# All tiles of a depthwise convolution as TensorE products, in a four-layer decoder trunk

## The chip, the cores and the metric

The kernel runs on one core of a Trainium2 chip. The metric is the device time of one launch in microseconds. A core has TensorE (PE, matrix products into PSUM), VectorE (DVE), ScalarE (ACT), GpSimd (POOL) and the sync engine (SP), which issues transfers. Each engine takes its instructions in order and waits on semaphores that others raise.

## The reference

Four pre-norm residual layers over 512 tokens of 1024 channels, in float32. Each is a token mixer followed by a squared-ReLU MLP of 4096 hidden channels; a last RMSNorm ends it. Layer 0 and 3 mix by sliding-window attention, layer 2 by a gated linear recurrence, layer 1 by the convolution module that the change touches:

```python
u = h @ w_pw1 + b_pw1                       # 1024 -> 2048
a, gate = jnp.split(u, 2, axis=-1)
u = a * jax.nn.sigmoid(gate)
c = causal_depthwise_conv(u, w_dw) + b_dw   # 31 taps, each channel by itself
c = jax.nn.silu(layer_norm(c, ln_g, ln_b))  # over the 1024 channels
return c @ w_pw2 + b_pw2
```

## The kernel before

Activations are kept transposed, channels on partitions: eight tiles of 128 channels by 512 tokens. Every large product is made of three matmuls on high and low parts of its operands; one such triple is a step (`step`, L271, matmuls at L277 to L279). After each step `pump` (L130) gives one turn to every live task, a Python generator whose `yield n` skips n turns. So tasks spread the work of other engines, and small TensorE products, among the steps; when the steps are over, `finish` (L140) gives turns until no task is left. This fixes the order in which instructions are written; a scheduler then orders each engine's list by that order and by when operands are expected to be ready. Weights are fetched ahead by the steps (`prefetch`, L256), rounded on ScalarE (wh) and subtracted on VectorE (wl), both at L254.

The convolution layer is `conformer` (L817). `linear` (L286) makes 16 output tiles of 8 steps, in pairs: for channel tile j first the gate, then the value. `glu` (L906) takes each from PSUM on VectorE (L909), applies the sigmoid on ScalarE (L912) and multiplies (L918). Then the tile goes one of two ways.

- Tiles 0 to 2 are convolved on VectorE by the task `on_dve` (L863): one ScalarE instruction for the last tap and 30 multiply-adds of the shifted tile (L872) each, written at a pace of one in 2.4 steps while steps last.
- Tiles 3 to 7 go to TensorE by a task `on_pe` (L887) each. Sixteen ScalarE copies (L891) bring the tile into a layout in which 32 channels by 4 neighbouring tokens lie on the partitions; after LAG (16) turns four groups follow, one per 32 channels. A group (`Convolution.group`, L807) is nine matmuls (L812) against a weight of 34 tap positions by 32 channels, three matmuls a turn; four ScalarE copies (L898) bring each group's result back.

The weights of a group are built on VectorE from a table of taps (`build`, L796, instruction at L802); the table is filled by `prepare` (L782, copies at L790), which starts after 16 turns and builds AHEAD (10) of them.

A shift per token, the mean of tile 0's channels (L856), is subtracted from all tiles (L860, L883, L901). `sums` (L832) adds each finished tile and its square to accumulators on GpSimd (L847, L848); the last but one to finish is added on VectorE, and its end starts `most`, which takes the means of the accumulators on TensorE (L393). The last one's means follow after `finish`. From them come mean and inverse deviation per token (L933 to L939), the normalised tiles (L954 to L958), and the projection `project` (L318), whose first step waits for the first of these.

Of the kernel before, what the change touches and what calls it, by code (L numbers as in the profile page):

```python
# [8 lines left out]
F32 = mybir.dt.float32  # L9
F32R = mybir.dt.float32r  # L10
I32 = mybir.dt.int32
AF = mybir.ActivationFunctionType
ALU = mybir.AluOpType
AX = mybir.AxisListType

P = 128
D = 1024
T = 512
KC = D // P
# [5 lines left out]
CW = 31  # L25
FF = 4 * D
EPS = 1e-6
SLAB = 256
CONV_ON_PE = 5
PACE = 2.4  # L30
LAG = 16
FAR = 1.0e34
W_BUFS = 5
U_BUFS = 3
# [18 lines left out]
def trunk_kernel(  # L53
# [7 lines left out]
    sc, ve, gp, pe = nc.scalar, nc.vector, nc.gpsimd, nc.tensor  # L61
# [12 lines left out]
    def ps_aux():  # L74
        return psa.tile([P, T], F32, tag="aux", name="aux")

    def scratch(name, shape=(P, T), dt=F32):
        return tmp.tile(list(shape), dt, tag="t", name=name)
# [18 lines left out]
    vrows = {}  # L97
# [18 lines left out]
    vecT = const.tile([P, KC, n_rows], F32, name="vecT")  # L116

    def vec(key, j, i=0):
        r = vrows[key] + i
        return vecT[:, j, r : r + 1]  # L120
# [3 lines left out]
    clock = [0]  # L124

    def spawn(gen):

        tasks.append([0, gen])
# [277 lines left out]
    class Norm:  # L406


        def __init__(self, key, i):
            self.key, self.i = key, i  # L410
            self.xs, self.r, self.r2 = [], None, None
            self.ms = tmp.tile([P, 2, NB], F32, tag="ms", name="ms", bufs=2)
            self.n = [0, 0]
# [350 lines left out]
    class Convolution:  # L764

        AHEAD = 10
        TAPS = CW + 3
        DIST = -(-TAPS // 4)  # L770

        def __init__(self):
            cp = self.pool = tc.tile_pool(name="cv", bufs=1)
            self.cp = cp.__enter__()
            self.built = []
            self.taps = self.cp.tile([P, CONV_ON_PE, 4, self.TAPS], F32, name="taps")
            self.i4 = self.cp.tile([P, 32], F32, name="i4")

        def close(self):
            self.pool.__exit__(None, None, None)  # L780

        def prepare(self):  # L782
            yield 16
            j0, r0 = KC - CONV_ON_PE, vrows["w_dw"]
            ve.tensor_reduce(self.i4, ident.rearrange("p (r c) -> p c r", r=4), AX.X, ALU.add)
            ve.memset(self.taps, 0.0)
            yield 2
            for g in range(4):
                for r in range(4):
                    ve.tensor_copy(self.taps[32 * r : 32 * r + 32, :, g, r : r + CW], vecT[32 * g : 32 * g + 32, j0:, r0 + CW - 1 : r0 - 1 : -1])  # L790
                yield 2
            for _ in range(self.AHEAD):
                self.build()
                yield 3

        def build(self):  # L796
            n = len(self.built)
            if n == 4 * CONV_ON_PE:
                return
            nx = self.TAPS  # L800
            w = self.cp.tile([P, nx, 32], F32, tag="w", name="w", bufs=self.AHEAD)
            ve.tensor_tensor(  # L802
                w, self.i4.unsqueeze(1).broadcast_to([P, nx, 32]), self.taps[:, n // 4, n % 4, :].unsqueeze(2).broadcast_to([P, nx, 32]), ALU.mult
            )
            self.built.append(w.rearrange("p x c -> p (x c)"))
# [9 lines left out]
                    yield 1  # L815

    def conformer(i, norm, nxt, conv):  # L817
        ON_DVE = KC - CONV_ON_PE
        cp = conv.cp
        cs, us = {}, {}  # L820
        done, parts, means, shared = [], [], {}, {}
        spawn(norm.inverse_root())

        def most():
            yield 6
            means["ps"] = ps_aux()
            token_means(means["ps"][:, :NB], shared["acc1"])
            token_means(means["ps"][:, NB : 2 * NB], shared["acc2"])
            means["most"] = tiny("most", 2 * NB)
            ve.tensor_copy(means["most"], means["ps"][:, : 2 * NB])  # L830

        def sums(j):  # L832

            done.append(j)
            if len(done) == 1:
                for k in ("acc1", "acc2"):
                    shared[k] = tmp.tile([P, T], F32, tag="acc", name=k, bufs=2)
                gp.tensor_copy(shared["acc1"], cs[j])
                sc.activation(shared["acc2"], cs[j], AF.Square)
                return  # L840
            sq = scratch("csq")
            sc.activation(sq, cs[j], AF.Square)
            if len(done) == KC:
                parts.extend((cs[j], sq))
                return
            e = ve if len(done) == KC - 1 else gp
            e.tensor_tensor(shared["acc1"], shared["acc1"], cs[j], ALU.add)  # L847
            e.tensor_tensor(shared["acc2"], shared["acc2"], sq, ALU.add)  # L848
            if len(done) == KC - 1:
                spawn(most())  # L850

        def first_shift():

            yield 4
            ps = ps_aux()
            pe.matmul(ps, ones, cs[0], start=True, stop=True)  # L856
            shift = shared["shift"] = tmp.tile([P, T], F32, tag="r", name="shift", bufs=2)
            sc.mul(shift, ps, 1.0 / P)
            yield 2
            ve.tensor_tensor(cs[0], cs[0], shift, ALU.subtract)  # L860
            sums(0)

        def on_dve():  # L863
            due = 0
            for j in range(ON_DVE):
                while j not in us:
                    yield 1
                c, u, b = cs[j], us[j], vec("b_dw", j)
                sc.activation(c, u, AF.Identity, scale=vec("w_dw", j, CW - 1), bias=b)
                for k in range(CW - 1):  # L870
                    late = CW - 1 - k
                    ve.scalar_tensor_tensor(c[:, late:], u[:, : T - late], vec("w_dw", j, k), c[:, late:], ALU.mult, ALU.add)  # L872
                    due = max(due + PACE, clock[0])
                    while clock[0] < due and len(us) < KC:
                        yield 1
                    if len(us) == KC:
                        yield 1
                if j == 0:
                    spawn(first_shift())
                    continue  # L880
                while "shift" not in shared:
                    yield 1
                ve.tensor_tensor(c, c, shared["shift"], ALU.subtract)  # L883
                sums(j)
                yield 1

        def on_pe(j, t):  # L887
            u = us[j].rearrange("p (g m) -> p g m", g=4)
            for g in range(4):
                for r in range(4):  # L890
                    sc.copy(u[32 * r : 32 * r + 32, g, :], t[32 * g : 32 * g + 32, r::4])  # L891
            yield LAG
            for g in range(4):
                ps = ps_aux()[:, :P]
                yield from conv.group(ps, 4 * (j - ON_DVE) + g, u[:, g, :])
                conv.build()
                for r in range(4):
                    sc.copy(cs[j][32 * g : 32 * g + 32, r::4], ps[32 * r : 32 * r + 32, :])  # L898
            while "shift" not in shared:
                yield 1  # L900
            ve.scalar_tensor_tensor(cs[j], cs[j], vec("b_dw", j), shared["shift"], ALU.add, ALU.subtract)  # L901
            sums(j)

        gates = {}

        def glu(n, ps):  # L906
            j, jj = n // 2, n % 2
            t = scratch("a")
            ve.tensor_tensor(t, ps, norm.factor(), ALU.mult)  # L909
            if jj == 0:  # L910
                gate = cp.tile([P, T], F32, name="gate", bufs=2)
                sc.activation(gate, t, AF.Sigmoid, bias=vec("b_pw1", j, 1))  # L912
                gates[j] = gate
                return
            uc = xcp.tile([P, 2, T], F32, tag="xc", name="uc")
            us[j], cs[j] = uc[:, 0, :], uc[:, 1, :]
            u = us[j] if j < ON_DVE else t
            ve.scalar_tensor_tensor(u, t, vec("b_pw1", j, 0), gates[j], ALU.add, ALU.mult)  # L918
            if j >= ON_DVE:
                spawn(on_pe(j, t))  # L920

        spawn(on_dve())
        linear(norm.xs, KC, glu, lead=KC - 1)
        for b in range(NB):
            gp.dma_start(out=rows[:, b, :], in_=conv_b_pw2[i].partition_broadcast(P), accum_op=ALU.add)
# [3 lines left out]
        ps = means["ps"]  # L929
# [237 lines left out]
    for c in range(XQ):  # L1167
        cs = slice(c * D // XQ, (c + 1) * D // XQ)
# [34 lines left out]
    for i in range(DEPTH):  # L1203
        mid = Norm("norm_mlp", i)
        if i % 3 == 0:
            attention(i // 3, norm, mid)
        elif i % 3 == 1:
            conv = Convolution()
            spawn(conv.prepare())
            conformer(i // 3, norm, mid, conv)  # L1210
            conv.close()
        else:
            hgrn(i // 3, i, norm, mid)
        norm = Norm("norm_mixer", i + 1) if i + 1 < DEPTH else None
        mlp(i, mid, norm)
# [31 lines left out]
```

## Time and profile before

| | us |
|---|---|
| median of three runs (2179.83 to 2183.03) | 2181.76 |
| the profiled execution | 2179.59 |
| its span, first to last instruction | 2177.8 |
| TensorE busy | 2122.2 |
| VectorE busy | 1418.3 |
| ScalarE busy | 1156.9 |
| GpSimd busy | 200.5 |

The profile is of one execution. Times of instructions are microseconds from the start of the span. TensorE's matmuls are pipelined: the durations of neighbours overlap, so the distance of their starts is what one costs. A float32 matmul appears as two records. PEld is the load of the stationary operand, which overlaps matmuls. PEclk is the clock that was granted to TensorE, as a share of the full 2.4 GHz, averaged over the stretch.

### The profile page before, as it was taken

How to read it: one execution, taken by the hardware profiler on the slowest of the kernel's cores; microseconds unless marked ns; L12 is line 12 of the kernel's file. 1: busy time of each engine (PE TensorE's matmuls, PEld its weight loads, DVE VectorE, ACT ScalarE, POOL GpSimd, SP SyncE). 2: the span in 40 equal slices, each digit the busy share in tenths (PEclk: the TensorE clock that was granted, in tenths of full speed). 3: DMA queues.
4: the chain of work that ended last, by engine and by line, in shares of the span. 5: the costliest groups of instructions: out<-in, count | busy, mean ns of one | idle time of the engine just before them, and what ended most of it. 6: DMA issues, size and time to landing. Idle time of an engine off the chain costs nothing.

```text
span 2177.8 us, 27270 instructions
## 1 busy us (share of the span) xinstructions
PE 2122.2 (97%) x10226; PEld 1742.0 (80%) x10226; DVE 1418.3 (65%) x2250; ACT 1156.9 (53%) x2015; POOL 200.5 (9%) x193
## 2 busy tenths in 40 slices
PE   7999999999988999999999999999999999999997
PEld 6778888888877888888788888888888878788886
DVE  5863754759986375574888874547558784547547
ACT  6755453455685445445555554544546684534545
POOL 0000110110020011011300000101100000101100
PEclk9999999999999999999999999999999999999999
DMA  4144756745214375674322226567564216567553
GB/s 149 49 146 111 187 117 157 177 84 126 78 40 135 97 174 110 170 172 94 87 66 78 77 70 174 111 169 173 109 170 88 61 48 195 114 158 177 120 129 77
DMA packets 211063, 262.56 MB, mean 121 GB/s; under 512 B 9027, under 2 KB 136003, under 8 KB 210932
## 3 DMA queue, kind: packets, MB, share of 16 engines
q1 hardware_dynamic: 175540, 191.61, 27.9%
q0 software_dynamic: 35392, 69.21, 20.1%
q8 instruction: 81, 1.33, 0.2%
q14 instruction: 50, 0.41, 0.1%
HBM read 258.69 MB, written 2.10 MB: 120 GB/s over the span
## 4 chain that ended last, share of the span: by engine, by line
PE 63%; DVE 18%; issue 8%; DMA 6%; ACT 5%; SPq 0%; POOL 0%; DVEq 0%; ACTq 0%; POOLq 0%
PE mm L279 18%; PE mm L278 18%; PE mm L277 18%; DVE wl L254 7%; DMA raw<-in_mlp_w_dram 5%; DVE rows L583 3%; DVE ul L544 2%; ACT wh L254 2%; PE aux L733 2%; PE aux L683 1%; PE aux L1047 1%; ACT uc L891 1%; DVE uc L872 1%; PE aux L428 1%; DVE us L538 1%
## 5 line engine op out<-in xcount | busy, mean ns | idle before, releaser
L254 DVE TENSOR_TENSOR wl<-raw,wh 128x1024 fp32r<-128x1024 f32 x452 | 552.7, 1223 | 532.5 <-ACT wh L254 530.1
L254 ACT CAST wh<-raw 128x1024 fp32r<-128x1024 f32 x452 | 468.7, 1048 | 497.3 <-DMA raw<-in_mlp_w_dram 198.3
L277 PE MATMUL mm<-x,wh 128*128 128x512 f32 x1568 | 630.6, 402 | 9.2 <-ACT wh L254 9.2
L279 PE MATMUL mm<-x,wl 128*128 128x512 f32 x1568 | 615.0, 392 | 7.6 <-DVE wl L254 7.6
L278 PE MATMUL mm<-x,wh 128*128 128x512 f32 x1568 | 613.4, 391 | 0.0
L279 PEld LDWEIGHTS mm<-x,wl 128*128 128x128 f32 x1568 | 294.7, 188 | 74.3 <-DVE wl L254 12.1
L277 PEld LDWEIGHTS mm<-x,wh 128*128 128x128 f32 x1568 | 295.4, 188 | 68.2 <-ACT wh L254 9.5
L278 PEld LDWEIGHTS mm<-x,wh 128*128 128x128 f32 x1568 | 295.6, 188 | 56.4 <-issue 1.4
L217 POOL DMA_DIRECT2D raw<-in_mlp_w_dram x128 | 153.5, 1206 | 1781.3 <-DVE wl L254 891.4
L277 PE MATMUL mm<-wh,uh 128*128 128x512 f32 x768 | 302.5, 394 | 7.1 <-DVE rows L583 4.7
L278 PE MATMUL mm<-wl,uh 128*128 128x512 f32 x768 | 299.2, 390 | 0.0
L279 PE MATMUL mm<-wh,ul 128*128 128x512 f32 x768 | 297.4, 390 | 0.3 <-DVE ul L544 0.3
L277 PEld LDWEIGHTS mm<-wh,uh 128*128 128x128 f32 x768 | 144.1, 188 | 45.8 <-DVE rows L583 7.5
L279 PEld LDWEIGHTS mm<-wh,ul 128*128 128x128 f32 x768 | 144.1, 188 | 31.2 <-DVE ul L544 0.8
L278 PEld LDWEIGHTS mm<-wl,uh 128*128 128x128 f32 x768 | 144.3, 188 | 28.0
L549 ACT ACTIVATE relu<-mm 128x512 f32<-128x512 f32 x128 | 75.9, 593 | 160.2 <-PE mm L279 160.2
L544 DVE TENSOR_TENSOR ul<-us,uh 128x1024 fp32r<-128x1024 f32 x64 | 78.2, 1222 | 32.5 <-ACT uh L543 32.5
L583 DVE SCALAR_TENSOR_TENSOR rows<-mm,nr,rows 128x512 f32<-128x512 f32 x128 | 95.8, 749 | 0.0
L550 ACT ACTIVATE us<-relu 128x512 f32<-128x512 f32 x128 | 81.0, 633 | 4.0
L277 PE MATMUL mm<-wh,y 128*128 128x512 f32 x192 | 77.6, 404 | 0.7 <-ACT y L358 0.7
L416 ACT ACTIVATE sq<-rows 128x512 f32<-128x512 f32 x64 | 40.2, 629 | 69.7 <-DVE rows L330 55.2
L279 PE MATMUL mm<-wh,y 128*128 128x512 f32 x192 | 76.2, 398 | 0.0
(232 smaller groups left out, 2559.5 us busy)
## 6 DMA issues: line engine op xcount, KB each, us to landing
raw<-in_mlp_w_dram SPq DMA_DIRECT2D x256, 512.0 KB
raw<-in_mlp_w_dram POOLq DMA_DIRECT2D x128, 512.0 KB, 6.1
raw<-in_hgrn_w_qfig_dram SPq DMA_DIRECT2D x64, 256.0 KB
raw<-in_attn_w_qkv_dram SPq DMA_DIRECT2D x20, 512.0 KB
raw<-in_attn_w_o_dram SPq DMA_DIRECT2D x16, 512.0 KB
raw<-in_conv_w_pw_dram SPq DMA_DIRECT2D x32, 256.0 KB
raw<-in_conv_w_pw_dram SPq DMA_DIRECT2D x8, 512.0 KB
raw<-in_hgrn_w_o_dram SPq DMA_DIRECT2D x8, 512.0 KB
```

The source lines that it names most:

```text
L217: gp.dma_start(out=wide(to), in_=block(w, r, c, h), accum_op=ALU.add)
L254: return sc.copy(wh, raw), ve.tensor_tensor(wl, raw, wh.bitcast(F32), ALU.subtract)
L277: pe.matmul(ps, sh, mh, start=start, stop=False, skip_group_check=again)
L278: pe.matmul(ps, sh, ml, start=False, stop=False, skip_group_check=again)
L279: pe.matmul(ps, sl, mh, start=False, stop=stop, skip_group_check=again)
L416: sc.activation(scratch("sq"), rows[:, b, f * T : (f + 1) * T], AF.Square, accum_out=self.ms[:, f, b : b + 1])
L428: pe.transpose(ps[:, b * P : (b + 1) * P], rows[:, b, j * P : (j + 1) * P], ident)
L544: ve.tensor_tensor(flat[1], src, flat[0].bitcast(F32), ALU.subtract)
L549: sc.activation(s, ps, AF.Relu)
L550: sc.activation(us[j // KH][:, :, j % KH, :], s.rearrange("p (h t) -> p h t", h=2), AF.Square)
L583: ve.scalar_tensor_tensor(o, banks[bank][p], norm.r2[sign][:, b : b + 1], o, ALU.mult, ALU.add)
L733: pe.matmul(po[h * HD : (h + 1) * HD, n * P : (n + 1) * P], vtok[:, n - 1 + b, kv * HD : (kv + 1) * HD], pT[:, b, n - n0, h, :], start=b = ...
```

## The change

All eight tiles go through `on_pe`; `on_dve`, the constant CONV_ON_PE and its pace are removed. The tap table and the weights cover eight tiles (32 builds instead of 20); 8 instead of 10 are built ahead, and the preparation starts after 4 turns instead of 16. LAG is 10 instead of 16. Of the sixteen layout copies of a tile those for the second and fourth 32 channels go to GpSimd; for the last tile half of the copies, into the layout and back, go to VectorE and half to ScalarE. Tile 0 gets its bias by a VectorE instruction of its own and starts the shift.

```diff
-CONV_ON_PE = 5
-PACE = 2.4
-LAG = 16
+LAG = 10
...
-        AHEAD = 10
+        AHEAD = 8
...
-            self.taps = self.cp.tile([P, CONV_ON_PE, 4, self.TAPS], F32, name="taps")
+            self.taps = self.cp.tile([P, KC, 4, self.TAPS], F32, name="taps")
...
-            yield 16
-            j0, r0 = KC - CONV_ON_PE, vrows["w_dw"]
+            yield 4
+            r0 = vrows["w_dw"]
...
-        def on_dve():
...
         def on_pe(j, t):
             u = us[j].rearrange("p (g m) -> p g m", g=4)
+            ends = j == KC - 1
             for g in range(4):
                 for r in range(4):
-                    sc.copy(u[32 * r : 32 * r + 32, g, :], t[32 * g : 32 * g + 32, r::4])
+                    o, src = u[32 * r : 32 * r + 32, g, :], t[32 * g : 32 * g + 32, r::4]
+                    if ends and r % 2:
+                        ve.tensor_copy(o, src)
+                    elif ends or g % 2 == 0:
+                        sc.copy(o, src)
+                    else:
+                        gp.tensor_copy(o, src)
             yield LAG
             for g in range(4):
                 ps = ps_aux()[:, :P]
-                yield from conv.group(ps, 4 * (j - ON_DVE) + g, u[:, g, :])
+                yield from conv.group(ps, 4 * j + g, u[:, g, :])
                 conv.build()
                 for r in range(4):
-                    sc.copy(cs[j][32 * g : 32 * g + 32, r::4], ps[32 * r : 32 * r + 32, :])
+                    o, src = cs[j][32 * g : 32 * g + 32, r::4], ps[32 * r : 32 * r + 32, :]
+                    if ends and r % 2:
+                        ve.tensor_copy(o, src)
+                    else:
+                        sc.copy(o, src)
+            if j == 0:
+                ve.tensor_scalar(cs[0], cs[0], vec("b_dw", 0), None, ALU.add)
+                spawn(first_shift())
+                return
...
-            u = us[j] if j < ON_DVE else t
-            ve.scalar_tensor_tensor(u, t, vec("b_pw1", j, 0), gates[j], ALU.add, ALU.mult)
-            if j >= ON_DVE:
-                spawn(on_pe(j, t))
-
-        spawn(on_dve())
+            ve.scalar_tensor_tensor(t, t, vec("b_pw1", j, 0), gates[j], ALU.add, ALU.mult)
+            spawn(on_pe(j, t))
+
         linear(norm.xs, KC, glu, lead=KC - 1)
```

## Rows read from the trace of the kernel before

**Rows 1.** The page, first part: busy time, share of the span, instructions.
```profile
PE 2122.2 (97%) x10226; PEld 1742.0 (80%) x10226; DVE 1418.3 (65%) x2250; ACT 1156.9 (53%) x2015; POOL 200.5 (9%) x193
```

**Rows 2.** Stretches: length, PE, PEld, DVE, ACT, POOL busy (x), clock, DMA.
```profile
506.40:626.70 120.30, 119.53 (x628) 99.58 (x627) 115.98 (x161) 74.29 (x146) 12.14 (x9) 1.00 0.34 88
626.70:636.10 9.40, 9.37 (x73) 8.07 (x71) 6.05 (x8) 7.44 (x14) 4.91 (x3) 1.00 0.13 34
636.10:645.00 8.90, 0.00 (x0) 0.00 (x0) 8.68 (x10) 7.81 (x20) 1.94 (x2) 0.79 0.24 82
645.00:657.50 12.50, 12.49 (x72) 10.69 (x72) 7.59 (x8) 9.78 (x25) 3.31 (x2) 0.74 0.01 1
657.50:673.80 16.30, 10.34 (x49) 10.03 (x48) 8.44 (x22) 5.56 (x11) 2.40 (x2) 0.69 0.81 267
```

**Rows 3.** The first stretch, instructions of L812 alone: PE, PEld busy.
```profile
506.40:626.70 120.30, 33.78 (x217) 30.32 (x218) 1.00 0.34 88
```

**Rows 4.** Timeline of TensorE, one group among steps: start, us, what.
```profile
563.58 0.39 PE L277 MATMUL mm<-x,wh 128*128 128x512 f32 x1
563.80 0.39 PE L278 MATMUL mm<-x,wh 128*128 128x512 f32 x1
564.03 0.39 PE L279 MATMUL mm<-x,wl 128*128 128x512 f32 x1
564.26 1.15 PE L812 MATMUL aux<-uc,w 128*128 128x128 f32 x6
...
568.68 1.15 PE L812 MATMUL aux<-uc,w 128*128 128x128 f32 x6
```

**Rows 5.** Timeline of all engines, 625 to 657 us.
```profile
626.36 0.39 PE L279 MATMUL mm<-x,wl 128*128 128x512 f32 x1
...
626.59 9.48 PE L812 MATMUL aux<-uc,w 128*128 128x128 f32 x72
...
633.50 0.68 DVE L909 TENSOR_TENSOR a<-mm,r 128x512 f32<-128x512 f32 x1
...
636.95 6.82 ACT L891 COPY uc<-a 32x128 f32<-32x128 f32 x16 [2.49 <-DVE a L918]
...
645.01 12.49 PE L812 MATMUL aux<-uc,w 128*128 128x128 f32 x72 [8.94 <-ACT uc L898]
```

**Rows 6.** Timeline of all engines, 657 to 674 us.
```profile
657.53 4.45 SPq L212 DMA_DIRECT2D raw<-in_mlp_w_dram  x8
657.54 1.55 ACT L898 COPY uc<-aux 32x128 f32<-32x128 f32 x4 [0.75 <-PE aux L812]
...
659.79 0.75 DVE L901 SCALAR_TENSOR_TENSOR uc<-uc,vecT,shift 128x512 f32<-128x512 f32 x1
659.91 1.29 ACT L842 ACTIVATE csq<-uc 128x512 f32<-128x512 f32 x2 [0.81 <-DVE uc L883]
...
661.28 3.16 PE L393 MATMUL aux<-ones_d,acc 128*128 128x1 f32 x16 [3.78 <-ACT csq L842]
...
666.49 1.85 PE L393 MATMUL aux<-ones_d,csq 128*128 128x1 f32 x8
668.37 0.16 DVE L933 TENSOR_TENSOR both<-most,aux 128x8 f32<-128x8 f32 x1 [3.73 <-PE aux L393]
...
673.80 0.50 PE L277 MATMUL mm<-wh,z 128*128 128x512 f32 x1 [1.58 <-ACT z L358]
```

**Rows 7.** VectorE by line: count, ns min/median/max, first and last start, forms.
```profile
L872 DVE SCALAR_TENSOR_TENSOR uc<-uc,vecT x90: 710/730/1748, 528.7 to 658.4; 128x482 f32<-128x482 f32 x3, 128x483 f32<-128x483 f32 x3, 128x484 f32<-128x484 f32 x3, 128x485 f32<-128x485 f32 x3
...
L802 DVE TENSOR_TENSOR w<-i,taps x20: 1274/1284/1293, 519.7 to 620.0; 128x1088 f32<-128x1088 f32 x20
...
L790 DVE COPY taps<-vecT x16: 236/249/329, 511.8 to 519.4; 32x155 f32<-32x155 f32 x16
```

**Rows 8.** GpSimd by line: the columns of the group before.
```profile
L838 POOL COPY acc<-uc x1: 1045/1045/1045, 584.6 to 584.6; 128x512 f32<-128x512 f32 x1
...
L847 POOL TENSOR_TENSOR acc<-acc,uc x5: 1270/1691/2128, 589.4 to 650.6; 128x512 f32<-128x512 f32 x5
```

More of the change, by code (lines that the diff above doesn't have):

```diff
@@ L789, in prepare @@
                 for r in range(4):
-                    ve.tensor_copy(self.taps[32 * r : 32 * r + 32, :, g, r : r + CW], vecT[32 * g : 32 * g + 32, j0:, r0 + CW - 1 : r0 - 1 : -1])
+                    ve.tensor_copy(self.taps[32 * r : 32 * r + 32, :, g, r : r + CW], vecT[32 * g : 32 * g + 32, :, r0 + CW - 1 : r0 - 1 : -1])
                 yield 2
@@ L797, in build @@
             n = len(self.built)
-            if n == 4 * CONV_ON_PE:
+            if n == 4 * KC:
                 return
@@ L817, in conformer @@
     def conformer(i, norm, nxt, conv):
-        ON_DVE = KC - CONV_ON_PE
         cp = conv.cp
@@ L861, in first_shift @@
             sums(0)
-        def on_dve():
[L864 to L885, printed above, removed]
         def on_pe(j, t):
             u = us[j].rearrange("p (g m) -> p g m", g=4)
+            ends = j == KC - 1
             for g in range(4):
                 for r in range(4):
-                    sc.copy(u[32 * r : 32 * r + 32, g, :], t[32 * g : 32 * g + 32, r::4])
+                    o, src = u[32 * r : 32 * r + 32, g, :], t[32 * g : 32 * g + 32, r::4]
[5 more added lines that the diff above has]
+                        gp.tensor_copy(o, src)
             yield LAG
```

## The prediction

> **What bounds the kernel now.** I read the page's share of each engine first, then a table of stretches around the convolution layer, then the order of work on TensorE, then the same stretches on all engines. The page says TensorE, 97% of the span [rows 1]; that is an average, and the layer of the change is where it fails. The table cuts that layer in five [rows 2]. From 506.4 to 626.7 us the pointwise product runs (16 output tiles of 8 steps, 3 matmuls each) and TensorE is busy 119.5 of 120.3 us, at the granted clock 1.00; VectorE is nearly full too (116 us), but nothing on TensorE waits for it. From 626.7 to 673.8 comes the tail, 47.1 us, in which TensorE does the products of the last two tiles and a few small sums, stands still for 8.9 us, and runs from 636.1 on at a mean clock of 0.69 to 0.79, that is partly at 1.2 instead of 2.4 GHz. So two prices hold here: before 626.7 each added TensorE product costs its full time and each VectorE instruction removed gives nothing; after it the latency of the chain from tile 7 to the next projection counts.
>
> **The price of a product.** The matmuls of the pointwise product start 0.22 to 0.23 us apart (563.58, 563.80), so three steps of three take 2.04 us. With one convolution group (9 matmuls, 18 records) put between three steps the next group starts 4.42 us later (564.26, 568.68) [rows 4]. A group costs 4.42 - 2.04 = 2.37 us; 72 records back to back, four groups, take 9.48 us, the same 2.37 each [rows 5]. In the long stretch there are 217 records, the twelve groups of tiles 3, 4 and 5 with one record over the edge [rows 3].
>
> The Trainium skill ("Perfetto Trace Analysis", Identifying the Most-Contended Engine) holds that matmul busy time says little of the headroom and that weight-load busy time is to be used; here that is 99.6 of 120.3 us [rows 2], and read so TensorE would have 20.7 us to spare. The rows say otherwise: weight loads overlap matmuls, and the interleaved group lengthened the stretch by its whole time [rows 4]. It stays as the first rival below.
>
> **What the change does, part by part.**
>
> 1. Three tiles go to TensorE: 12 groups more, 12 x 2.37 = 28.4 us. Their 90 VectorE instructions of about 0.73 us [rows 7], some 65 us, vanish, with three ScalarE starts and two subtractions. In the long stretch that gives nothing, TensorE being full. It matters only in the tail, where the last 14 or so of them ran between the steps of tiles 6 and 7.
>
> 2. LAG falls from 16 to 10 task turns, and a step of the product is one turn. Tile 6 is spawned 16 steps before the last, so its groups start 11 steps later and two of its four lie in the long stretch; before, all four lay behind. That makes 26 groups in the long stretch instead of 12: 14 x 2.37 = 33.1 us. One stall of about 0.8 us there (the difference of span and busy time, [rows 2]) should go with the shorter ScalarE batches. The last pointwise matmul, 626.36 before [rows 5], comes 32.3 us later, at about 659.
>
> 3. Behind it six groups remain, 6 x 2.37 = 14.2 us, at full clock if nothing pauses. The 16 small means over the first seven tiles now fall among them, since tile 6 is then the last but one in order and no VectorE tile is awaited; they took about 3.2 us at the lower clock [rows 6], so 1.6 to 3.2; I take 1.6, the engine being warm. The last group ends at 659 + 14.2 + 1.6 = 675 us; before it ended at 657.5 [rows 2]. That is 17.4 later.
>
> 4. Does tile 7 arrive in time? Before, its scaling on VectorE began 7.1 us after the start of the last matmul (633.50), its sixteen copies on ScalarE lasted from 636.95 to 643.77, and TensorE resumed at 645.01 after 8.94 us of idleness, at half speed: 12.49 us for the 72 records that take 9.48 warm [rows 5]. Both losses, 8.9 + 3.0 = 11.9 us, are in the 47.1. In the new order the two last groups of tile 6 occupy TensorE for 4.7 us. Against that stand scaling and gating (0.68 + 0.75, durations as of the rows for such 512-column instructions, [rows 5, 6]) and for the first group two ScalarE copies of 0.43 us beside two on VectorE, about 2.5 us, if ScalarE and VectorE are free; older evacuations and weight casts in their queues can add 2 or 3. So the 11.9 us go, nearly or wholly. Behind ScalarE's copies for tile 7 queue tile 6's last evacuations; they decide when the means of point 3 may start.
>
> 5. The end of the chain. Before: four evacuations (1.55 us), subtraction at 659.79, then VectorE's two additions, 16 + 8 + 8 means, the statistics at 668.37 and the projection at 673.80 [rows 6]: 16.3 us from the last group. After: two copies on each of two engines, about 0.95 us until the subtraction; 0.75 for it, 0.65 for the square (two take 1.29) with an estimated 0.2 of hand-over; eight means at 0.9 (half of the 1.85 shown, at twice the clock) to 1.85 us; 0.1 to the statistics, then the same 5.43 us. That is 0.95 + 8.0 to 8.95 = 9 to 9.9 us, or 6.4 to 7.3 less.
>
> 6. GpSimd takes 8 of 16 layout copies of tiles 0 to 6, so ScalarE's share falls by 3.4 us per tile. No row shows GpSimd copying 32x128. Nearest above: its 128x512 copy, 1.05 us; an addition with two inputs, 2.13 at worst [rows 8]; below, nothing. A tile lasts 16 x 0.68 + 9.5 = 20.4 us on TensorE now. At 0.5 us the eight copies are 4 us and hidden by the turns of LAG, some 11 us with the neighbour's groups in them; cost taken: 0. At up to 2.1 us (20.4 less 3.6 for the two additions, over 8) it still keeps up.
>
> 7. The tap tables: 16 copies of 248 instead of 155 columns (0.26 us each now), a longer clearing, 32 instead of 20 weight builds at 1.28 us [rows 7]. On a VectorE that lost 65 us the 12 x 1.28 = 15.4 us are covered in the long stretch. At its start they are not: preparation is moved 12 turns ahead, up to four more builds (5.1 us) and about 2.5 us of longer copies stand ahead of the operands of the first tiles. Tile 0's groups are wanted 11 steps after its product, and the shift waits for all four. If the instruction order lets pointwise steps go first, this costs nothing; else up to 6 us. I take 1 here and 1 for small waits at point 4, both near their lower ends, because TensorE has 100 us of other steps to run first.
>
> Sum: 17.4 - 6.9 + 2 = 12.5 us. The weight loads for the next MLP's sums, eight on the sync queue, wait for the convolution's memory, which the last group frees (657.53, [rows 6]); they start some 17 us later with it, yet are wanted only after 128 steps, 87 us, from the projection's start, and GpSimd's own transfers follow them. So everything behind the projection moves by the same amount. The profiled execution's own time is 2179.6 us (span 2177.8 and 1.8 around it): 2192.1. The median of the runs is 2.2 above that execution; carried over, 2194.3. **I predict 2194 us, slower.**
>
> **Rivals.**
> - *The added products fit in TensorE's gaps* (not slower). For it: 20.7 us of the long stretch without a weight load [rows 2]. If these took up the fourteen added groups, 2194.3 - 20.7 = 2174 us; it decides from the point where an added group costs under 2.37 - 12.5/14 = 1.48 us. Against it: each interleaved group cost 2.37 [rows 4]. This is what the Trainium skill's rule on weight loads would give. Chance 4%; a half of it, about no change, 3%.
> - *Tile 7 is late again* (slower still). ScalarE and VectorE work in order; if older evacuations, a table load or weight casts delay its layout as they did, the 8.9 us of idleness and 3.0 of half clock come back [rows 5]: 2194.3 + 11.9 = 2206 us. Against it: eight ScalarE copies instead of sixteen, no tap instructions on VectorE. Chance 11%, parts of it being within the forecast's range.
> - *GpSimd becomes the bound.* At 2.5 us a copy it needs 8 x 2.5 + 3.6 = 23.6 us per tile against 20.4; seven tiles fall behind by 22 us: 2216. For it: its additions vary from 1.27 to 2.13 us beside a busy VectorE [rows 8]. Against it: the copy has a quarter of the columns of the 1.05 us one, and VectorE is freer. Chance 4%. The Trainium skill (same page, Optimizing Scalar/DVE Operations) warns that work moved between GpSimd and VectorE may not help since they share a read port; no row here shows it for copies.
> - The forecast: 78%, its own range 2188 to 2203 (no stall and a faster tail, to 8 us of stalls more).
>
> **How the numbers follow.** What a measurement tells from no change is about 0.2%, 4.4 us. The 80% range takes the forecast's own and stops short of the rivals: 2187 to 2205. Faster 4%, same 4%, slower 92%.
>
> **What would show it.** Right: the last pointwise matmul near 659 us, convolution groups still 2.37 us apiece, the last one ending at 675 to 679, at clock 1.00, the projection at 684 to 690, VectorE's busy time in the layer down by about 50 us without use. Wrong: three steps with a group taking less than 4.4 us; a pause of several us before tile 7's first group; GpSimd busy without a gap; a projection before 680.

## The result, and the profile after

The changed kernel takes 2200.91 us (median of six runs, 2198.07 to 2206.63) against 2181.41 (2179.83 to 2183.03): ratio 1.0093, 95% interval 1.0082 to 1.0104. It is 19.5 us slower; the forecast was 12.5 us slower, and the time lies inside its range of 2187 to 2205. The profiled execution took 2201.09 us, its span 2199.0.

The page's first part, which answers to [rows 1]:

```profile
PE 2151.6 (98%) x10442; PEld 1767.5 (80%) x10442; DVE 1376.0 (63%) x2189; ACT 1161.9 (53%) x2036; POOL 235.7 (11%) x249
```

TensorE is busy 29.4 us more, VectorE 42.3 less: work moved from an engine with room to the one without. The table of stretches of the layer, cut at the same events as [rows 2] (columns as there: length, busy time of PE, PEld, DVE, ACT, POOL, granted clock, DMA):

```profile
506.33:661.05 154.72, 152.28 (x873) 127.49 (x872) 90.39 (x107) 95.10 (x200) 57.55 (x71) 1.00 0.27 72
661.05:669.86 8.81, 8.81 (x67) 7.50 (x65) 4.71 (x11) 8.54 (x20) 0.00 (x0) 1.00 0.21 60
669.86:671.98 2.12, 0.01 (x1) 0.03 (x1) 1.56 (x3) 1.21 (x4) 0.00 (x0) 0.94 0.00 0
671.98:675.81 3.83, 3.83 (x18) 3.83 (x19) 0.95 (x2) 0.56 (x2) 0.00 (x0) 0.50 0.02 4
675.81:684.70 8.89, 8.87 (x47) 7.88 (x47) 2.10 (x6) 1.51 (x4) 0.00 (x0) 0.65 0.00 0
684.70:695.04 10.34, 5.94 (x33) 5.59 (x33) 5.67 (x17) 4.16 (x8) 0.00 (x0) 0.70 0.87 318
```

The first line is the long stretch, 154.7 us where it was 120.3. The projection starts at 695.04, where [rows 6] had 673.80: 21.2 us later, the whole difference of the spans. So the layer holds all of it. Within the long stretch a group costs what it did; the first third of one group and of the next, with three steps between them, start 4.41 us apart (4.42 in [rows 4]):

```profile
642.03 1.15 PE L810 MATMUL aux<-uc,w 128*128 128x128 f32 x6
646.44 1.15 PE L810 MATMUL aux<-uc,w 128*128 128x128 f32 x6
```

The tail is 34.0 us where it was 47.1, so it gave back 13.1 of the 34.4 us by which the long stretch grew. Its order on TensorE (start, us, what, idle time before it and its releaser):

```profile
660.82 0.40 PE L277 MATMUL mm<-x,wl 128*128 128x512 f32 x1
661.05 8.81 PE L810 MATMUL aux<-uc,w 128*128 128x123 f32 x66
671.98 1.83 PE L391 MATMUL aux<-ones_d,acc 128*128 128x1 f32 x8 [2.12 <-DVE acc L844]
673.68 0.77 PE L810 MATMUL aux<-uc,w 128*128 128x126 f32 x2
674.25 1.71 PE L391 MATMUL aux<-ones_d,acc 128*128 128x1 f32 x8
675.81 8.87 PE L810 MATMUL aux<-uc,w 128*128 128x125 f32 x46
687.26 1.02 PE L391 MATMUL aux<-ones_d,uc 128*128 128x1 f32 x8 [2.58 <-DVE uc L889]
...
695.04 0.80 PE L275 MATMUL mm<-wh,z 128*128 128x512 f32 x1 [1.58 <-ACT z L356]
```

Tile 7 is not late: its groups follow tile 6's without a gap, 66 records in 8.81 us. But the 16 means of the accumulators (L391) now stand among them, and TensorE, in order, waits 2.12 us for VectorE's addition L844. After that gap the granted clock is 0.50, the lower level; the last 46 records, at a mean clock of 0.65, take 8.87 us, where at 2.37 us for 18 they would take 6.06. The addition is late because of ScalarE's order: tile 6's last evacuations (L882) stand behind tile 7's layout copies (L869), and the shift's subtraction on VectorE (L889) waits for them.

```profile
663.68 3.44 ACT L869 COPY uc<-a 32x128 f32<-32x128 f32 x8
667.14 3.12 ACT L882 COPY uc<-aux 32x128 f32<-32x128 f32 x8
670.29 0.75 DVE L889 SCALAR_TENSOR_TENSOR uc<-uc,vecT,shift 128x512 f32<-128x512 f32 x1 [4.07 <-ACT uc L882]
671.14 0.69 DVE L844 TENSOR_TENSOR acc<-acc,uc 128x512 f32<-128x512 f32 x1
```

The other wait of the layer is at its start, all TensorE waits between 505 and 720 us being these (waiting, released by: us in total, times, longest):

```profile
PE aux L391 <- DVE uc L889: 2.6, 1, 2.6
PE aux L381 <- DVE y L374: 2.2, 1, 2.2
PE aux L391 <- DVE acc L844: 2.1, 1, 2.1
PE mm L275 <- ACT z L356: 1.6, 1, 1.6
PE aux L810 <- ACT uc L869: 0.3, 1, 0.3
PE aux L381 <- DVE both L918: 0.3, 1, 0.3
```

The spread of the norm's inverse root (L381) waits 2.2 us. The timeline of VectorE says why: the root's chain of tiny instructions (L446, L370 to L374) sits among the tap copies that now start 12 turns earlier.

```profile
516.00 1.23 DVE L252 TENSOR_TENSOR wl<-raw,wh 128x1024 fp32r<-128x1024 f32 x1
517.26 1.17 DVE L788 COPY taps<-vecT 32x248 f32<-32x248 f32 x4
518.44 0.16 DVE L446 TENSOR_TENSOR v<-ms 128x4 f32<-128x4 f32 x1
...
520.54 1.28 DVE L800 TENSOR_TENSOR w<-i,taps 128x1088 f32<-128x1088 f32 x1
521.75 0.15 DVE L374 SCALAR_TENSOR_TENSOR y<-t,y 128x4 f32<-128x4 f32 x1
```

GpSimd's new copies and its additions, by line (busy us, mean ns, idle before):

```profile
L871 POOL COPY uc<-a 32x128 f32<-32x128 f32 x56 | 39.8, 710 | 56.2 <-DVE a L905 54.1
L844 POOL TENSOR_TENSOR acc<-acc,uc 128x512 f32<-128x512 f32 x5 | 6.4, 1286 | 19.5 <-DVE uc L889 19.5
```

A copy takes 0.71 us in the mean (most take 0.40, as the last section shows), and GpSimd is idle between tiles, waiting for the tile (L905): it is no bound.

### The profile page after: what moved, and what is told of

It reads as the page before. It is cut to its first block, busy times and chain, and to the rows that moved or that the text cites. A ratio compares the mean times of both kernels' runs of the same rounds, so it can differ in the third digit from the quotient of the medians.

```text
span 2199.0 us, 27738 instructions
## 1 busy us (share of the span) xinstructions
PE 2151.6 (98%) x10442; PEld 1767.5 (80%) x10442; DVE 1376.0 (63%) x2189; ACT 1161.9 (53%) x2036; POOL 235.7 (11%) x249
## 4 chain that ended last, share of the span: by engine, by line
PE 67%; DVE 16%; issue 7%; DMA 6%; ACT 4%; SPq 0%; POOL 0%; DVEq 0%; ACTq 0%; POOLq 0%
PE mm L277 19%; PE mm L276 19%; PE mm L275 19%; DVE wl L252 7%; DMA raw<-in_mlp_w_dram 5%; DVE rows L581 3%; PE aux L810 3%; DVE ul L542 2%; ACT wh L252 2%; PE aux L731 2%; PE aux L681 1%; PE aux L1032 1%; PE aux L426 1%; DVE us_sum L533 1%; DVE us L536 1%
## 5 line engine op out<-in xcount | busy, mean ns | idle before, releaser
L810 PEld LDWEIGHTS aux<-uc,w 128*128 128x128 f32 (+1 forms) x576 | 80.5, 191 | 16.6 <-issue 5.4
L810 PE MATMUL aux<-uc,w 128*128 128x128 f32 (+8 forms) x576 | 90.5, 289 | 0.3 <-ACT uc L869 0.3
L275 PE MATMUL mm<-wh,y 128*128 128x512 f32 x192 | 77.7, 404 | 0.7 <-ACT y L356 0.7
```

Source lines behind the costliest of these rows:

```text
L275: pe.matmul(ps, sh, mh, start=start, stop=False, skip_group_check=again)
L810: pe.matmul(ps[: m.shape[1], d:], m, u[:, : P - d], start=k == 0, stop=k == self.DIST - 1)
```

## The experiments

The theory going in: in the long stretch TensorE is full, each added group costs its whole time, and the tail gave part of its gain back to a wait inside tile 7's groups and the clock that fell after it. Rivals: the products fit into gaps between weight loads; the moved schedule (LAG, preparation, GpSimd), not the number of products, is the loss. "Less" below is against the changed kernel's 2200.9 us. Intervals are of ratios to the kernel before, which was run again with each set of experiments (medians 2180.1 to 2181.65 us); the changed kernel's own is 1.0082 to 1.0104.

**Products left out (thin).** Tiles 0 to 2 run three of the nine matmuls of each group: the loop's index k goes from 0 to 8, and the edit skips 2 to 7. The expectation counts seven left out; it is six.

```diff
             for k, d in enumerate(order):
+                if n < 12 and 2 <= k < self.DIST - 1:
+                    if k % 3 == 2:
+                        clock[0] += 1
+                        yield 1
+                    continue
```

> Tiles 0 to 2 keep their task turns, copies and weights, but each of their twelve groups runs 2 of its 9 matmuls (7 of 9 left out, so the convolution of these tiles is incomplete). If every added product costs its full time on a full TensorE: 12 x 7/9 x 2.37 = 22 us less than the changed kernel, about 2179 us, with the long stretch shorter by 22 us. If the products fit into gaps of the weight loads: less than 5 us, 2196 to 2201. If the copies, the taps or GpSimd set the pace: no change.

Measured: 2185.01 us, 15.9 less; ratio 1.0022 (1.0013 to 1.0032). That is neither 22 nor under 5, and with six left out the full price would be 12 x 6/9 x 2.37 = 19.0, so the trace has to decide. One thinned group among three steps, and the start of the next (a matmul is two records):

```profile
537.93 0.73 PE L815 MATMUL aux<-uc,w 128*128 128x128 f32 x4
...
540.09 0.38 PE L815 MATMUL aux<-uc,w 128*128 128x121 f32 x2
...
541.01 0.73 PE L815 MATMUL aux<-uc,w 128*128 128x128 f32 x4
```

From group to group 3.08 us instead of 4.42: 1.34 us were removed, not 6/9 of 2.37, which is 1.58. Why the three matmuls that stay cost 1.04 us and not a third of 2.37 is not shown. 12 x 1.34 = 16.1 us, against 15.9 measured, so the time that left TensorE's order is returned one to one. The idea of room between weight loads falls: they cover 127.5 of 154.7 us in the changed kernel, and the matmuls did not fit into the rest.

**The means later (most_late).**

```diff
         def most():
-            yield 6
+            yield 18
```

> The small means over the first seven tiles are written 18 instead of 6 turns after the seventh tile, behind tile 7's last group. If the wait for VectorE's accumulators inside tile 7's groups, and the half clock after it, are what the tail lost: the 2.1 us of idleness go, the clock stays at 2.4 GHz through tile 7, 16 means fill the wait for tile 7's copies: 6 to 9 us less, 2192 to 2195. If TensorE's clock falls anyway and the means only move: 0 to 2 us less, 2199 to 2201.

Measured: 2197.26 us, 3.6 less; ratio 1.0075 (1.0063 to 1.0088), the runs from 2194.3 to 2199.1. Less than expected, and the interval touches that of the changed kernel. The profiled run, 2194.26 us, shows the mechanism:

```profile
661.16 14.81 PE L810 MATMUL aux<-uc,w 128*128 128x123 f32 x114
675.81 1.85 PE L391 MATMUL aux<-ones_d,acc 128*128 128x1 f32 x16
```

All 114 records run without a gap at full clock, and the projection starts at 689.19, 5.9 us earlier. The table of stretches shows what stays:

```profile
661.16:675.81 14.65, 14.65 (x116) 12.97 (x114) 8.77 (x19) 11.66 (x28) 0.00 (x0) 1.00 0.12 37
675.81:677.66 1.85, 1.85 (x18) 1.76 (x16) 0.39 (x1) 0.61 (x2) 0.00 (x0) 1.00 0.22 44
677.66:689.19 11.53, 7.32 (x32) 6.97 (x32) 5.83 (x18) 3.79 (x7) 0.37 (x1) 0.54 0.96 357
```

After a 2.4 us wait for the last tile the final chain runs at a mean clock of 0.54. Why the timed runs gain less than the profiled one is open; the profiled one had the highest mean clock over its whole span, 0.996 against 0.991 to 0.994 in the other four.

**LAG as before (lag16).**

```diff
-LAG = 10
+LAG = 16
```

> LAG back at 16 turns, all else as changed. If the number of products sets the time: the two groups of tile 6 move from the long stretch to behind it, 4.7 us from one side to the other, 2199 to 2203. If a late tile 7 was the price that LAG 10 saved: the idleness of 8.9 us and the cold clock return, 2208 to 2213. If a short LAG is what hurts: under 2197.

Measured: 2200.25 us, ratio 1.0095 (1.0080 to 1.0111): no difference. The trace shows the groups moved as expected, 96 records between the last step and the wait instead of 66, and the same wait after them:

```profile
657.19 12.80 PE L810 MATMUL aux<-uc,w 128*128 128x128 f32 x96
672.08 1.84 PE L391 MATMUL aux<-ones_d,acc 128*128 128x1 f32 x8 [2.10 <-DVE acc L844]
```

Tile 7 is in time with either LAG; what made it late before the change was not LAG alone.

**No copies on GpSimd (no_pool).**

```diff
                     else:
-                        gp.tensor_copy(o, src)
+                        sc.copy(o, src)
```

> All layout copies of tiles 0 to 6 on ScalarE, none on GpSimd. If GpSimd's copies hide behind the task turns and TensorE is full: within 2 us of the changed kernel, 2199 to 2203. If ScalarE then delays the evacuations: 2203 to 2208. If GpSimd's slow copies were the bound: 2190 or less.

Measured: 2201.79 us, ratio 1.0096 (1.0082 to 1.0109): no difference. Sharing the copies bought and cost nothing, since ScalarE had room: with all the copies it is busy 117.8 of 155.5 us in the long stretch.

**Preparation as late as before (prep16).**

```diff
         def prepare(self):
-            yield 4
+            yield 16
```

> The tap preparation starts after 16 turns, as before the change. If moving it ahead put its copies before the chain of the norm's inverse root on VectorE, the wait of 2.2 us before the spread at the start of the long stretch goes: 1.5 to 2.5 us less than the changed kernel, 2198 to 2199.5, with the last pointwise matmul that much earlier against the first. If the first groups then lack their weights: the 2.2 us come back as a wait for them, no change.

Measured: 2199.0 us, 1.9 less, ratio 1.0084 (1.0069 to 1.0099), so not separable by the times. In its trace the wait of L381 is gone, tile 0's first group waits 1.1 instead of 0.3 us, and from the first pointwise matmul to the last the stretch takes 152.9 instead of 154.5 us, 1.6 less, as expected:

```profile
519.41 1.05 PE L381 MATMUL aux<-ident,y 128*128 128x128 f32 x8
529.78 1.25 PE L810 MATMUL aux<-uc,w 128*128 128x128 f32 x6 [1.12 <-ACT uc L869]
```

**Tiles back on VectorE (mix1, mix2, mix3).** The changed kernel with the task of before for its first one, two or three tiles.

```diff
+N_DVE = 1        # 2, 3
+PACE = 2.4
...
+        def on_dve():            # as before the change, for j in range(N_DVE)
...
+            u = us[j] if j < N_DVE else t
+            if j >= N_DVE:
+                spawn(on_pe(j, t))
```

> The changed kernel with tile 0 convolved on VectorE as before the change (31 instructions at the old pace), seven tiles on TensorE. If a tile on TensorE costs its full time: 9.5 us less, 2190 to 2193. If the schedule of the tail and not the number of tiles sets the time: 2198 to 2202.

> Tiles 0 and 1 on VectorE, six on TensorE, all else as changed. If each tile costs its full time on TensorE and VectorE keeps up: 19 us less than the changed kernel, 2180 to 2184, about the time before the change, with two tiles less of VectorE work than half a stretch. If VectorE's products delay tile 7: 2186 or more.

> Tiles 0 to 2 on VectorE as before, with the changed kernel's LAG, GpSimd copies, early preparation and split last tile. If only the number of products made the change slow and these parts repair the tail of before: 2170 to 2177, below the time before. If VectorE's last tile (its products ended at 658 before) closes the stretch: 2178 to 2183, the time before. If these parts are themselves the loss: 2190 or more.

Measured: 2192.97 (ratio 1.0059, 1.0044 to 1.0074), 2180.06 (0.9993, 0.9984 to 1.0003) and 2184.81 us (1.0017, 1.0007 to 1.0026): 7.9, 20.8 and 16.1 less. The first two tiles return 10.4 us each on average, near the 9.5 of four groups; in the traces the first to the last pointwise matmul takes 154.5, 146.4 and 136.7 us with none, one and two of them on VectorE, 8.9 less each. The third tile returns nothing, and mix3, a little slower than the kernel before, lies between its second and third branch: the changed kernel's other parts do not repair that tail. VectorE then ends last; the waits of TensorE in mix3 between 505 and 700 us, of which the first two are the new ones:

```profile
PE aux L393 <- ACT csq L841: 8.7, 1, 8.7
PE aux L812 <- DVE uc L893: 4.7, 1, 4.7
```

The second is tile 7's layout, copied on VectorE behind the tap products; the first is the end, where the last product on VectorE starts at 662.2 us. So the time turns at two tiles on VectorE.

**A version that beats both (best_late, best_mid).** Two tiles on VectorE, the preparation after 16 turns, the means 18 or 12 turns later.

```diff
 # mix2, and
-            yield 4       # prepare
+            yield 16
...
-            yield 6       # most
+            yield 18      # best_mid: 12
```

> Two tiles on VectorE and six on TensorE, the preparation after 16 turns, the means of the first seven tiles 18 turns after the seventh. If the three effects seen singly add up (19 or 20 us from the two tiles, 2 from the preparation, 3 to 6 from the means): 2173 to 2177, below the time before. If the clock or VectorE takes the later ones back: 2178 to 2182.

> The same with the means 12 turns after the seventh tile, in the middle of tile 7's groups, when VectorE's accumulators should be ready. If only the wait on them matters: like the one with 18 turns or up to 1.5 us less, as the means are then out of the last chain. If any small matmul between the groups costs by itself: 1 to 3 us more than that one.

Measured: best_late 2171.72 us, ratio 0.9962 (0.9949 to 0.9974), 29 us under the changed kernel and 9.5 under the one before. best_mid 2175.08, ratio 0.9972 (0.9962 to 0.9982): 3.4 us more than best_late, nearest to the last branch, though the two intervals overlap. It waits 0.6 us for VectorE before the means. The 16 means then take 1.78 us at clock 1.00, and the last 12 records run at a mean clock of 0.58. Of all TensorE waits in the layer best_late keeps these:

```profile
PE aux L393 <- DVE uc L915: 2.4, 1, 2.4
PE mm L277 <- ACT z L358: 2.1, 3, 1.6
PE aux L383 <- DVE both L947: 0.3, 1, 0.3
```

The single effects (20.8, 1.9 and 3.6) add up to 26.3 of the 29.2 us.

## Why the prediction was right, and where it was short

Direction and mechanism held: a full TensorE, each group at its whole price, VectorE's 65 us worth nothing. Of its own signs of being right, those of the tail did not come: the last group ended at 684.7 and not by 679, its clock was not 1.00, and the projection came at 695 and not by 690. The time fell inside the range because that allowed for up to 8 us of stalls. The size, 21.3 us from the first pointwise matmul to the projection against 12.5 forecast, differs by these terms:

- *Points 1 and 2, the long stretch.* Forecast: the last pointwise matmul 32.3 us later; measured 34.5 (626.36 in [rows 5], 660.82 after). The group's price was right. Two waits, 2.2 us at L381 and 0.3 at the first group, were added; against them 246 records more, 13.7 groups and not 14, fell into the stretch, 0.8 us less; some 0.5 us are not assigned. Point 7 saw that the early preparation stands ahead of the first tiles' operands, without naming the norm's root, and put it at 1 us, reasoning that TensorE has other steps to run. It cannot run them: the spread stands between the steps in its order, and prep16 removes that wait, if for 0.8 us of another.
- *Points 3 and 4, behind the last pointwise matmul.* Forecast: all groups and means done at about 675; measured 684.7. From 660.82 on that is 23.9 us instead of 16, 7.9 of the 8.8 missing. Point 4's worry, a late tile 7, did not occur. The last sentence of point 4, that tile 6's last evacuations decide when the means may start, was the real one, and got one microsecond for all waits there. It cost 2.1 us of idleness, 2.2 for the means (3.8 instead of 1.6, "the engine being warm") and 2.8 for the groups at the lower clock; the other 0.8 us are the third of a group, 114 records and not 108, that lay behind the last step. most_late removed the first three in its trace. The mis-sized term is the warm clock. How much it costs changes from run to run: the same wait, 2.10 to 2.13 us, stands in lag16, no_pool, thin, mix1, prep16 and mix2, and from its end to the last group pass 12.8, 11.2, 11.2, 11.2, 9.6 and 9.6 us, here 12.7; most_late's rates would give 7.7. So the lower clock cost an estimated 1.9 to 5.1 us, and this profile is near the upper end.
- *Point 5, the last chain.* Forecast 9 to 9.9 us; measured 10.3. The two copies on each of two engines were to take 0.95 us until the subtraction; they took 1.65:

```profile
684.72 0.37 ACT L882 COPY uc<-aux 32x128 f32<-32x128 f32 x1 [1.13 <-PE aux L810]
685.12 0.38 DVE L880 COPY uc<-aux 32x128 f32<-32x128 f32 x1 [1.10 <-ACT uc L882]
685.53 0.37 ACT L882 COPY uc<-aux 32x128 f32<-32x128 f32 x1 [0.44 <-DVE uc L880]
685.94 0.39 DVE L880 COPY uc<-aux 32x128 f32<-32x128 f32 x1 [0.44 <-ACT uc L882]
```

  Each waits for the other engine's, so they run one after another, and splitting them gained nothing: the four took 1.55 us on ScalarE alone [rows 6]. Tile 7's layout copies did run side by side (ScalarE from 663.68, VectorE from 663.97). Those write different rows from SBUF; these write interleaved columns of the same rows from one PSUM tile. Which of the two orders them is not shown.
- *Point 6, GpSimd.* Right: 0.71 us a copy in the mean, and no effect without it.
- *The rivals.* Room between weight loads fell with thin; tile 7 late and GpSimd as the bound fell with the trace and no_pool.

Together 2.2 + 7.9 + 0.9 less the 2 us allowed give 9.0, the 8.8 missing but for rounding.

## What to carry to other kernels

Moving work to an engine that is busy without a gap costs the full price of the work, however idle it makes another; look at the busy time of the stretch, not of the kernel, and balance until the other engine would end last, here at two of eight tiles. Small products that wait for another engine do not belong in the middle of a dense run of other products: put them behind it, where the engine waits anyway. (The traces of most_late and best_late show this; in the times it is 3 to 4 us, with intervals that overlap.) A split of copies over two engines gains only if the copies are not ordered one after another.

## What the runs showed of the hardware that was not expected

A gap of 2.12 us on TensorE, after a stretch at clock 1.00, was followed by 3.8 us at 0.50 and 8.9 us at a mean of 0.65, although the engine was busy throughout both. All seven profiles with this gap show a loss of clock behind it, but not at once in each: in prep16 the means still ran at 1.00, and only the last 46 records fell to a mean of 0.77. In most_late and best_late, with no gap, the groups and the means ran at 1.00. The one-column means always follow the gap of 2.1 us, so what each of the two does to the clock is not told apart.

GpSimd's 32x128 copies were held up beside VectorE. Of the 56 the median takes 0.40 us, the longest 3.88. Those over 1 us between 529 and 538 and between 643 and 648 us each start under a VectorE instruction with two input tensors and end some 0.3 us behind it or the last of a row, here three weight builds:

```profile
529.02 3.68 DVE L800 TENSOR_TENSOR w<-i,taps 128x1088 f32<-128x1088 f32 x3
529.09 3.88 POOL L871 COPY uc<-a 32x128 f32<-32x128 f32 x1
533.01 0.40 POOL L871 COPY uc<-a 32x128 f32<-32x128 f32 x1
```

So the third rival's ground, a GpSimd slowed beside VectorE, is seen for copies too; as no_pool shows, it cost TensorE nothing.
